# A two-layer encoder on one core: the taps of a depthwise convolution move between two engines, and the first weights are rounded on another one

## The chip, the core and the metric

The kernel runs on one core of a Trainium2 chip. The core has a matrix engine (TensorE, in the profile PE, with its weight loads as PEld), a vector engine (VectorE, DVE), an engine for functions of one operand (ScalarE, ACT), a general engine (GpSimd, POOL) and a queue for transfers (SyncE, SP). Each engine works through its own queue of instructions in a fixed order and waits where it needs something from another one. The metric is device time in microseconds, from the start of the program to its end; the median of three runs counts.

## The reference, cut to what matters

Two layers, 256 tokens, 2048 channels, float32. The attention part (two head groups and one output projection) is the same before and after. The change lies in the second half of each layer:

```python
def depthwise_conv(u, w, bias):                 # u: (1, 256, 11264), w: (3, 11264)
    up = jnp.pad(u, ((0, 0), (1, 1), (0, 0)))
    return up[:, :-2] * w[0] + up[:, 1:-1] * w[1] + up[:, 2:] * w[2] + bias

h2 = rms_norm(x, ln2_g[l])
u = depthwise_conv(h2 @ w_up[l], conv_w[l], conv_b[l])
gate, up = u[..., :D_FF], u[..., D_FF:]         # D_FF = 5632
x = x + (jax.nn.silu(gate) * up) @ w_down[l]
```

## The kernel before, in words

**Weights in two parts.** Every float32 weight tile (`raw`, 128x2048, 1 MB) comes in by a transfer on SP's queue and is split in two halves of 1024 columns. ACT rounds a half to a high part `whi` (line 112), DVE subtracts this from the weight to get the low part `wlo` (line 113), and PE multiplies with both. `split_w` (line 752) does this four steps ahead of PE (`SPLIT_AHEAD`), with five buffers for each part: the rounding of a step can start when PE has left the buffer of five steps before. `x` and all other activations are split in the same way (lines 112 to 117; `mid` tiles hold both parts of one activation).

**The feed-forward half of a layer.** The 5632 hidden channels are 44 pieces of 128 (gate and up together). A piece is made by two weight tiles (`q_up`, line 527), four steps of PE, and then `glu` (line 541) on the other engines: ACT copies one half of the result out of PSUM (545), DVE adds the other half (546) and scales it by the row norm into a tile `halo` with room for the neighbours (547), POOL copies the two edges (549, 550). The convolution is next: ACT computes the middle tap with the bias, once for the gate and once for up (555), and DVE adds the two neighbours' taps to each, four instructions with multiply and add in one (557). ACT applies SiLU (559), DVE multiplies with the other half (561), and the result is split into a `mid` tile (563). After every second piece `sums_mid` (570) makes sums and differences of the two (574 to 577) and splits those too.

**Five groups of pieces.** The pieces go in groups of 8, 8, 8, 8 and 12 (`CHUNKS`). After the ninth `q_up` of a group comes `q_plain` (639), whose result DVE adds to `x` (654), and then four times a `seven` tile followed, in the first four groups, by a `down` tile. A `seven` tile holds four weight blocks of a product that is built from seven block products; its three parts are split in `split_seven` (743), where DVE first combines the blocks in place (747, 748, 749): part 1 needs 747, part 2 needs 749. So with every `seven` tile ACT waits for DVE, DVE for ACT, and PE for both.

**What sets the order.** The code is recorded by a framework whose scheduler sorts the instructions of each engine by its own estimate of their times and by priorities; `split_w` has a priority ahead of the other work. An engine's order can therefore move far from an edit. Buffers: `pT` tiles (`y` in `glu`) are four in turn.

**The start.** `head` (norm weights and the first two blocks of x transposed) and the next two blocks come on ACT's queue, the first weight tile in four parts and the second one on SP's queue. ACT rounds the blocks of x (`first_x`, line 786, by way of 115) and the first weights (112), each in program order.

Of the kernel before, what the change touches and what calls it, by code (L numbers as in the profile page):

```python
# [11 lines left out]
F32 = mybir.dt.float32  # L12
F32R = mybir.dt.float32r
I32 = mybir.dt.int32
AF = mybir.ActivationFunctionType
ALU = mybir.AluOpType
AX = mybir.AxisListType

P = 128
L = 2  # L20
T = 256
# [10 lines left out]
NF = FF // P  # L32
# [27 lines left out]
def encoder_kernel(  # L60
# [5 lines left out]
    nc = tc.nc  # L66
# [3 lines left out]
    work = ctx.enter_context(tc.tile_pool(name="work", bufs=2))  # L70
# [38 lines left out]
    def split(hi, lo, src, scale=None):  # L109

        if scale is None:
            high = nc.scalar.activation(hi, src, AF.Copy)  # L112
            nc.vector.tensor_sub(lo, src, hi.bitcast(F32))  # L113
        else:
            high = nc.scalar.activation(hi, src, AF.Copy, scale=scale)  # L115
            nc.vector.scalar_tensor_tensor(lo, src, scale, hi.bitcast(F32),
                                           op0=ALU.mult, op1=ALU.subtract)
        return high
# [10 lines left out]
    def prep_x(l, which, k, src):  # L129

        xs[k] = act.tile([P, 2, T], F32R, name=f"xs{k}")
        split(xs[k][:, 0], xs[k][:, 1], src, ln_g[:, which, l, k:k + 1])
# [385 lines left out]
    def middle(l, f):  # L518

        name, bufs = "mid", MIDS  # L520
        if f >= NF - CHUNKS[-1]:
            k = count[l] = count.get(l, 0) + 1
            if k > MIDS:
                name, bufs = SPARE[k - MIDS - 1]
        return act.tile([P, 2, T], F32R, name=name, bufs=bufs)

    def q_up(l, f, u):
        def body(q, half, hi, lo):
            if u == 0 and half == 0:
                cur["up"] = psum.tile([P, 2, 2, T], F32, name="mm", bufs=2)  # L530
            ps = cur["up"]
            hv, lv = (w.rearrange("p (k j n) -> p k j n", k=4, j=2) for w in (hi, lo))
            for j in range(2):
                for kk in range(4):
                    k = 8 * u + 4 * half + kk
                    two(ps[:, j], hv[:, kk, j], lv[:, kk, j], xs[k], k == 0, k == KD - 1)
            if u == 1 and half == 1:
                glu(l, f, ps)
        return body

    def glu(l, f, ps):
        ux = halo[f % 2]
        r = T // GRID_W
        t = work.tile([P, 2, T], F32, name="prob", bufs=2)
        nc.scalar.activation(t, ps[:, :, 0], AF.Copy)  # L545
        nc.vector.tensor_add(t, t, ps[:, :, 1])  # L546
        nc.vector.tensor_mul(ux[:, :, r:r + T], t, st["r2"][:, None, :].to_broadcast([P, 2, T]))  # L547

        nc.gpsimd.tensor_copy(ux[:, :, 1:r], ux[:, :, T:T + r - 1])  # L549
        nc.gpsimd.tensor_copy(ux[:, :, T + r:T + 2 * r - 1], ux[:, :, r + 1:2 * r])  # L550
        y = work.tile([P, 2, T], F32, name="pT", bufs=4)
        for j in range(2):
            c = j * NF + f
            w0, w1, w2, b = (par["conv"][:, l, i, c:c + 1] for i in range(4))
            nc.scalar.activation(y[:, j, :], ux[:, j, r:r + T], AF.Identity, scale=w1, bias=b)  # L555
            for w, o in ((w0, 0), (w2, 2 * r)):
                nc.vector.scalar_tensor_tensor(y[:, j, :], ux[:, j, o:o + T], w, y[:, j, :],  # L557
                                               op0=ALU.mult, op1=ALU.add)
        nc.scalar.activation(t[:, 0, :], y[:, 0, :], AF.Silu)  # L559
        m = work.tile([P, T], F32, name="bias", bufs=2)  # L560
        nc.vector.tensor_mul(m, t[:, 0, :], y[:, 1, :])
        gs[f] = middle(l, f)
        split(gs[f][:, 0], gs[f][:, 1], m)
        ms[f] = m
        if f % 2 and f < NF - CHUNKS[-1] + PART:
            sums_mid(l, f // 2, ms.pop(f - 1), ms.pop(f))
# [3 lines left out]
    def sums_mid(l, p, m1, m2):  # L570

        a, b = slice(0, P), slice(P, T)
        v = work.tile([P, 4, HD], F32, name="tq", bufs=2)
        nc.vector.tensor_add(v[:, 0], m1[:, b], m2[:, b])
        nc.vector.tensor_sub(v[:, 1], v[:, 0], m1[:, a])
        nc.vector.tensor_sub(v[:, 2], m1[:, a], m1[:, b])
        nc.vector.tensor_sub(v[:, 3], m2[:, a], v[:, 1])
        for i in range(2):
            t = middle(l, 2 * p)
            split(t[:, 0], t[:, 1], v[:, 2 * i:2 * i + 2].rearrange("p j n -> p (j n)"))  # L580
            for j in range(2):
                ss[p, 2 * i + j] = t[:, :, j * P:(j + 1) * P]
# [116 lines left out]
    for l in range(L):  # L699
# [7 lines left out]
        f = 0  # L707
# [25 lines left out]
    raw, hl, left, loads, highs = {}, {}, {}, {}, {}  # L733

    def load(q, parts=1):
        if q < len(quanta):
            raw[q] = wp.tile([P, 2048], F32, name="raw", bufs=3)
            left[q] = 3 if quanta[q][2] == "seven" else 2
            m = 2048 // parts
            for j in range(parts):  # L740
                loads[q] = nc.sync.dma_start(out=raw[q][:, j * m:(j + 1) * m], in_=quanta[q][0][:, j * m:(j + 1) * m])

    def split_seven(w, part, hi, lo):

        hv, lv = (t.rearrange("p (k n) -> p k n", k=2) for t in (hi, lo))
        if part == 1:
            nc.vector.tensor_sub(w[:, 1:3], w[:, 1:3], w[:, 2:4])
            nc.vector.tensor_add(w[:, 3], w[:, 3], w[:, 1])
            nc.vector.tensor_sub(w[:, 0], w[:, 3], w[:, 0])
        return split(hv, lv, (w[:, 1::2], w[:, 1:3], w[:, 0::3])[part])  # L750

    def split_w(s, parts=1):
        if s < len(steps):
            q, half = steps[s]
            kind = quanta[q][2]
            o = UP_AT if kind == "up" else 0
            hl[s] = tuple(wp.tile([P, 1024 + 64], F32R, name=t, bufs=SPLIT_AHEAD + 1)[:, o:o + 1024]
                          for t in ("whi", "wlo"))
            with tc.high_priority(offset=AHEAD_PRIO if s >= KD // 2 else 0):
                if kind == "seven":  # L760
                    highs[s] = split_seven(raw[q].rearrange("p (k n) -> p k n", k=4), half, *hl[s])
                else:
                    m = 1024 // parts
                    for j in range(parts):
                        highs[s] = split(*(t[:, j * m:(j + 1) * m] for t in hl[s]),
                                         raw[q][:, half * 1024 + j * m:half * 1024 + (j + 1) * m])
            left[q] -= 1
            if left[q] == 0:
                del raw[q]
                load(q + LOAD_AHEAD)  # L770
# [15 lines left out]
    def first_x(i):  # L786
        for j in range(2):
            prep_x(0, 0, 2 * i + j, xT[i][:, j, :])
# [7 lines left out]
    par = {}  # L796
# [37 lines left out]
        mm(ps[:, 0:P], ones, ones, True, True)  # L834

    for i in range(SPLIT_AHEAD):
        first_x(i)
        split_w(i, 2 if i == 0 else 1)
    for n, shape, dt, src in (
            ("pos", [P, TT], I32, a["pos"]),  # L840
            ("inv", [P, HD // 2], F32, a["inv"].partition_broadcast(P))):
# [11 lines left out]
    for s, (q, half) in enumerate(steps):  # L853
        if s + SPLIT_AHEAD < KD // 2:
            first_x(s + SPLIT_AHEAD)
        split_w(s + SPLIT_AHEAD)
        quanta[q][1](q, half, *hl.pop(s))
        for f, args in side.pop((q, half), []):
            f(*args)
# [101 lines left out]
```

## Time and profile before

| | us |
|---|---|
| median of three runs | 2092.12 |
| lowest and highest | 2092.11, 2092.13 |
| the profiled execution, its own time | 2092.0 |
| its span, first to last instruction | 2090.2 |
| PE busy in the span | 2083.5 |
| DVE busy | 1720.5 |
| ACT busy | 1222.3 |
| POOL busy | 170.3 |

The span is read from left to right; a window of it is given in microseconds from its start. The granted clock of PE is 1.00 over the whole span. One feed-forward half has five groups that look alike in the trace: nine pieces of `q_up`, in which DVE and ACT have much idle time, and then some 34 us of `q_plain`, `seven` and `down`, in which DVE is nearly always busy. A row of a timeline gives start, busy time, engine, line, operation, what it writes and reads, and in brackets the idle time before it and what ended that; neighbouring instructions of one kind are merged with their count.

### The profile page before, as it was taken

Reading aid. Unit: us, or ns where it says so; the run is one execution under the profiler, and the core shown is the slowest. Engines: PE = TensorE matmul, PEld = TensorE weight load, DVE = VectorE, ACT = ScalarE, POOL = GpSimd, SP = SyncE. Lnnn points to the kernel's source line nnn. Section 1 sums busy time; section 2 is a strip of 40 time slices with the busy share of each in tenths; the row PEclk is TensorE's granted clock in tenths of the full one; section 3 lists DMA queues with packets and bytes.
Section 4 is the critical chain, followed back from the end, with each engine's and each line's share of the span. In section 5 each row is a group of like instructions: output and inputs, shape, how many; then the busy total and the mean of one; then the engine's idle time right before and its main releaser. Section 6 shows DMA issues by size and latency. Waiting matters only on the chain.

```text
span 2090.2 us, 29185 instructions
## 1 busy us (share of the span) xinstructions
PE 2083.5 (100%) x10816; PEld 1789.2 (86%) x10816; DVE 1720.5 (82%) x2604; ACT 1222.3 (58%) x1817; POOL 170.3 (8%) x237
## 2 busy tenths in 40 slices
PE   9999999999999999999999999999999999999999
PEld 8888888888888888888888888888888888888887
DVE  7786757898898988989757866678989989899896
ACT  7566556555555556556555665565556555555563
POOL 0011100100101001010000011001001010010100
PEclk9999999999999999999999999999999999999999
DMA  9544555556565564655655444555555655556554
GB/s 350 199 145 164 179 172 174 198 195 211 180 241 182 208 210 167 242 193 211 208 181 181 162 160 166 177 182 189 214 202 170 236 199 204 201 185 234 185 200 161
DMA packets 62144, 408.42 MB, mean 195 GB/s; under 512 B 7344, under 2 KB 9904, under 8 KB 13744
## 3 DMA queue, kind: packets, MB, share of 16 engines
q1 hardware_dynamic: 61280, 405.46, 56.2%
q8 instruction: 85, 1.39, 0.3%
q10 hardware_dynamic: 720, 1.08, 0.2%
q14 instruction: 59, 0.48, 0.1%
HBM read 404.42 MB, written 2.10 MB: 194 GB/s over the span
## 4 chain that ended last, share of the span: by engine, by line
PE 99%; DMA 0%; ACT 0%; DVE 0%; issue 0%
PE mm L98 90%; PE S L98 4%; PE pv L98 3%; PE tr L98 2%; PE tr L373 1%; PE tr L307 1%; PE S L149 1%; DMA head<-in_head 0%; ACT qtok L274 0%; ACT kT L315 0%; ACT xs L115 0%; DVE x L688 0%; ACT whi L112 0%
## 5 line engine op out<-in xcount | busy, mean ns | idle before, releaser
L112 ACT ACTIVATE whi<-raw 128x1024 fp32r<-128x1024 f32 (+1 forms) x797 | 830.9, 1057 | 689.9 <-PE mm L98 411.9
L113 DVE TENSOR_TENSOR wlo<-raw,whi 128x1024 fp32r<-128x1024 f32 (+1 forms) x797 | 963.9, 1220 | 270.3 <-ACT whi L112 231.8
L98 PE MATMUL mm<-xs,whi 128*128 128x512 f32 x2816 | 977.0, 390 | 0.0
L98 PE MATMUL mm<-xs,wlo 128*128 128x256 f32 x2816 | 794.1, 282 | 0.0
L98 PEld LDWEIGHTS mm<-xs,whi 128*128 128x128 f32 x2816 | 528.3, 188 | 110.5
L98 PEld LDWEIGHTS mm<-xs,wlo 128*128 128x128 f32 x2816 | 532.2, 189 | 1.1
L98 PE MATMUL mm<-whi,mid 128*128 128x512 f32 x1412 | 368.2, 391 | 0.0
L98 PEld LDWEIGHTS mm<-whi,mid 128*128 128x128 f32 x1412 | 263.0, 188 | 53.9
L98 PE MATMUL mm<-whi,xs 128*128 128x512 f32 x1152 | 294.2, 393 | 1.4 <-ACT qtok L274 1.3
L98 PEld LDWEIGHTS mm<-whi,xs 128*128 128x128 f32 x1152 | 213.1, 188 | 44.7 <-ACT qtok L274 1.8
L98 PE MATMUL mm<-wlo,mid 128*128 128x512 f32 x706 | 202.4, 392 | 0.0
L98 PE MATMUL mm<-wlo,xs 128*128 128x512 f32 x576 | 159.5, 393 | 0.0
L98 PEld LDWEIGHTS mm<-wlo,mid 128*128 128x128 f32 x706 | 132.1, 188 | 27.0
L557 DVE SCALAR_TENSOR_TENSOR pT<-halo,conv,pT 128x256 f32<-128x256 f32 x352 | 148.1, 478 | 0.9
L549 POOL COPY halo<-halo 128x6 f32<-128x6 f32 x88 | 39.6, 450 | 1232.6 <-DVE halo L547 1232.6
L98 PEld LDWEIGHTS mm<-wlo,xs 128*128 128x128 f32 x576 | 107.3, 188 | 21.6
L555 ACT ACTIVATE pT<-halo,conv 128x256 f32<-128x256 f32 x176 | 95.1, 587 | 5.8 <-DVE halo L547 5.7
L550 POOL COPY halo<-halo 128x6 f32<-128x6 f32 x88 | 77.1, 876 | 0.2 <-POOL halo L549 0.2
L547 DVE TENSOR_TENSOR halo<-prob,acc_b 128x512 f32<-128x512 f32 x88 | 60.6, 689 | 1.9
L546 DVE TENSOR_TENSOR prob<-prob,mm 128x512 f32<-128x512 f32 x88 | 59.8, 679 | 0.0
L545 ACT ACTIVATE prob<-mm 128x512 f32<-128x512 f32 x88 | 51.3, 583 | 7.1 <-PE mm L98 7.1
L559 ACT ACTIVATE prob<-pT 128x256 f32<-128x256 f32 x88 | 35.5, 404 | 30.0 <-DVE pT L557 30.0
(180 smaller groups left out, 1475.4 us busy)
## 6 DMA issues: line engine op xcount, KB each, us to landing
raw<-in_w_up SPq DMA_DIRECT2D x176, 1024.0 KB, 4.9
raw<-in_w_in SPq DMA_DIRECT2D x71, 1024.0 KB, 4.9
raw<-in_w_down SPq DMA_DIRECT2D x48, 1024.0 KB, 4.8
raw<-in_w_seven SPq DMA_DIRECT2D x40, 1024.0 KB, 4.9
raw<-in_w_out SPq DMA_DIRECT2D x32, 1024.0 KB, 4.9
raw<-in_w_plain SPq DMA_DIRECT2D x10, 1024.0 KB, 4.8
bias<-in_bias SPq DMA_DIRECT2D x16, 160.0 KB, 3.1
x<-in_x SPq DMA_DIRECT2D x4, 512.0 KB, 10.7
```

What stands on the lines that cost most here:

```text
L98: nc.tensor.matmul(ps, lhsT, rhs, start=start, stop=stop, skip_group_check=True)
L112: high = nc.scalar.activation(hi, src, AF.Copy)
L113: nc.vector.tensor_sub(lo, src, hi.bitcast(F32))
L149: nc.tensor.transpose(ps[:, j, tt * P:(tt + 1) * P], x[:, tt, (k + j) * P:(k + j + 1) * P], ident)
L545: nc.scalar.activation(t, ps[:, :, 0], AF.Copy)
L546: nc.vector.tensor_add(t, t, ps[:, :, 1])
L547: nc.vector.tensor_mul(ux[:, :, r:r + T], t, st["r2"][:, None, :].to_broadcast([P, 2, T]))
L549: nc.gpsimd.tensor_copy(ux[:, :, 1:r], ux[:, :, T:T + r - 1])
L550: nc.gpsimd.tensor_copy(ux[:, :, T + r:T + 2 * r - 1], ux[:, :, r + 1:2 * r])
L555: nc.scalar.activation(y[:, j, :], ux[:, j, r:r + T], AF.Identity, scale=w1, bias=b)
L557: nc.vector.scalar_tensor_tensor(y[:, j, :], ux[:, j, o:o + T], w, y[:, j, :], op0=ALU.mult, op1=ALU.add)
L559: nc.scalar.activation(t[:, 0, :], y[:, 0, :], AF.Silu)
```

## The change

The neighbours' taps: ACT now multiplies each tap by its weight (four instructions of 256 columns in a piece), into two further `pT` tiles `z`, and DVE adds a whole `z` (gate and up, 512 columns) to `y` in one instruction, twice in a piece. Before, DVE did four instructions of 256 columns. The very first weight half: DVE rounds it (two copies of 512 columns) instead of ACT, and ACT's rounding of the first two blocks of x stands after these in the program.

```diff
+        w = [[par["conv"][:, l, i, j * NF + f:j * NF + f + 1] for i in range(4)] for j in range(2)]
         for j in range(2):
-            c = j * NF + f
-            w0, w1, w2, b = (par["conv"][:, l, i, c:c + 1] for i in range(4))
-            nc.scalar.activation(y[:, j, :], ux[:, j, r:r + T], AF.Identity, scale=w1, bias=b)
-            for w, o in ((w0, 0), (w2, 2 * r)):
-                nc.vector.scalar_tensor_tensor(y[:, j, :], ux[:, j, o:o + T], w, y[:, j, :],
-                                               op0=ALU.mult, op1=ALU.add)
+            nc.scalar.activation(y[:, j, :], ux[:, j, r:r + T], AF.Identity, scale=w[j][1], bias=w[j][3])
+        for i, o in ((0, 0), (2, 2 * r)):
+            z = work.tile([P, 2, T], F32, name="pT", bufs=4)
+            for j in range(2):
+                nc.scalar.activation(z[:, j, :], ux[:, j, o:o + T], AF.Copy, scale=w[j][i])
+            nc.vector.tensor_add(y, y, z)
         nc.scalar.activation(t[:, 0, :], y[:, 0, :], AF.Silu)
...
-                    m = 1024 // parts
-                    for j in range(parts):
-                        highs[s] = split(*(t[:, j * m:(j + 1) * m] for t in hl[s]),
-                                         raw[q][:, half * 1024 + j * m:half * 1024 + (j + 1) * m])
+                    w = raw[q][:, half * 1024:(half + 1) * 1024]
+                    if s == 0:
+                        m = [slice(j * 512, (j + 1) * 512) for j in range(2)]
+                        for j in m:
+                            highs[s] = nc.vector.tensor_copy(hl[s][0][:, j], w[:, j])
+                        first_x(0)
+                        with tc.issue_after(highs[s].ins):
+                            for j in m:
+                                nc.vector.tensor_sub(hl[s][1][:, j], w[:, j], hl[s][0][:, j].bitcast(F32))
+                    else:
+                        highs[s] = split(*hl[s], w)
```

In the changed kernel's line numbers the middle tap is 554, a neighbour's tap on ACT 559, DVE's addition 560, SiLU 561, the product 563; `q_plain`'s addition is 656 and the three block combinations are 749, 750 and 751.

The scheduler also gives other orders at the end of each group. **DVE, from the addition of the ninth piece's two halves to the combinations of the second `seven` tile.** `prob` and `halo` are the ninth piece's, `x<-x,mm` is `q_plain`'s addition, `tq` and `mid` the sums of pieces seven and eight. Before:

```order
L546 TENSOR_TENSOR prob<-prob,mm 128x512
L113 TENSOR_TENSOR mid<-tq,mid 128x256
L547 TENSOR_TENSOR halo_110<-prob,acc_b 128x2x256
L113 TENSOR_TENSOR wlo<-raw,whi 128x1024
L654 TENSOR_TENSOR x<-x,mm 128x512
L113 TENSOR_TENSOR wlo<-raw,whi 128x1024
L113 TENSOR_TENSOR mid<-tq,mid 128x256
L113 TENSOR_TENSOR wlo<-raw,whi 128x1024
L557 SCALAR_TENSOR_TENSOR pT<-halo_110,conv,pT 128x256 x2
```

Now:

```order
L546 TENSOR_TENSOR prob<-prob,mm 128x512
L113 TENSOR_TENSOR mid<-tq,mid 128x256
L656 TENSOR_TENSOR x<-x,mm 128x512
L547 TENSOR_TENSOR halo_110<-prob,acc_b 128x2x256
L113 TENSOR_TENSOR wlo<-raw,whi 128x1024 x3
L113 TENSOR_TENSOR mid<-tq,mid 128x256
L113 TENSOR_TENSOR wlo<-raw,whi 128x1024
L560 TENSOR_TENSOR pT<-pT 128x512
```

`q_plain`'s addition to `x`, which waits for PE, now stands ahead of 547 and of the low part of the first `seven` tile's last part.

**DVE, the rows that follow, through the second `seven` tile.** Before:

```order
L113 TENSOR_TENSOR wlo<-raw,whi 128x1024
L557 SCALAR_TENSOR_TENSOR pT<-halo_110,conv,pT 128x256 x2
L747 TENSOR_TENSOR raw<-raw 128x1024
L561 TENSOR_TENSOR bias<-prob,pT 128x256
L748 TENSOR_TENSOR raw<-raw 128x512
L749 TENSOR_TENSOR raw<-raw 128x512
L113 TENSOR_TENSOR wlo<-raw,whi 128x1024
```

Now:

```order
L749 TENSOR_TENSOR raw<-raw 128x1024
L560 TENSOR_TENSOR pT<-pT 128x512
L750 TENSOR_TENSOR raw<-raw 128x512
L113 TENSOR_TENSOR wlo<-raw,whi 128x1024
L751 TENSOR_TENSOR raw<-raw 128x512
L563 TENSOR_TENSOR bias<-prob,pT 128x256
```

The last combination (749 before, 751 now), for which part 2's rounding waits, now stands behind a low part of 1024 columns.

**PE, parts 1 and 2 of that second `seven` tile.** `whi_4131` and `whi_4144` are the high parts of parts 1 and 2 before, `whi_4167` and `whi_4180` now; `wlo_4132` and `wlo_4168` are part 1's low parts. Before:

```order
L98 MATMUL S_4112<-whi_4131,mid_3534 128x512 x2
L98 MATMUL S_4111<-whi_4131,mid_3531 128x512 x2
L98 MATMUL pv_4114<-whi_4144,mid_3523 128x512 x2
L98 MATMUL mm_4110<-whi_4144,mid_3531 128x512 x2
L98 MATMUL S_4112<-wlo_4132,mid_3534 128x512
```

Now:

```order
L98 MATMUL S_4148<-whi_4167,mid_3550 128x512 x2
L98 MATMUL S_4147<-whi_4167,mid_3547 128x512 x2
L98 MATMUL S_4148<-wlo_4168,mid_3550 128x512
L98 MATMUL S_4147<-wlo_4168,mid_3547 128x512
L98 MATMUL pv_4150<-whi_4180,mid_3539 128x512 x2
```

The two products with part 1's low part now come ahead of part 2's first product.

## Rows read from the trace of the kernel before

**Rows 1.** The page, part 1: engine, busy us (share of the span), instructions.

```profile
PE 2083.5 (100%) x10816; PEld 1789.2 (86%) x10816; DVE 1720.5 (82%) x2604; ACT 1222.3 (58%) x1817; POOL 170.3 (8%) x237
```

**Rows 2.** Waits of PE: who waited for whom, us, times, longest.

```profile
PE mm L98 <- ACT qtok L274: 1.3, 2, 0.7
PE pv L98 <- DVE halfpi L94: 1.1, 1, 1.1
```

**Rows 3.** Busy time by window; columns PE, PEld, DVE, ACT, POOL, clock, DMA.

```profile
434.00:468.00 34.00, 34.00 (x152) 28.15 (x151) 33.63 (x37) 20.08 (x24) 1.18 (x2) 1.00 0.58 208
468.00:564.00 96.00, 96.00 (x546) 84.66 (x545) 84.23 (x129) 56.25 (x81) 8.76 (x15) 1.00 0.58 201
```

**Rows 4.** Chain that ended last, in order of time: the first pieces of two groups.

```profile
467.87 94.66 PE mm L98 x538
...
597.44 94.66 PE mm L98 x538
```

**Rows 5.** Groups by line and form: the removed taps, the nearest form on ACT.

```profile
L557 DVE SCALAR_TENSOR_TENSOR pT<-halo,conv,pT 128x256 f32<-128x256 f32 x352 | 148.1, 478 | 0.9
L115 ACT ACTIVATE xs<-mid,head 128x256 fp32r<-128x256 f32 x14 | 6.0, 495 | 0.1
```

**Rows 6.** Timeline of DVE, eighth piece of a group, up to its `seven` tile.

```profile
424.81 1.67 DVE L557 SCALAR_TENSOR_TENSOR pT<-halo,conv,pT 128x256 f32<-128x256 f32 x4
426.43 1.23 DVE L113 TENSOR_TENSOR wlo<-raw,whi 128x1024 fp32r<-128x1024 f32 x1
```

**Rows 7.** Timeline of ACT there, the middle taps and the next rounding.

```profile
423.54 1.08 ACT L555 ACTIVATE pT<-halo,conv 128x256 f32<-128x256 f32 x2
425.34 1.06 ACT L112 ACTIVATE whi<-raw 128x1024 fp32r<-128x1024 f32 x1 [0.72 <-ACT pT L555]
```

**Rows 8.** Timeline of POOL there: the edges.

```profile
423.69 1.26 POOL L550 COPY halo<-halo 128x6 f32<-128x6 f32 x1
```

**Rows 9.** Timeline of DVE, from the ninth piece's scaling to the second `seven` tile.

```profile
433.26 0.68 DVE L547 TENSOR_TENSOR halo<-prob,acc_b 128x512 f32<-128x512 f32 x1
433.86 1.22 DVE L113 TENSOR_TENSOR wlo<-raw,whi 128x1024 fp32r<-128x1024 f32 x1
435.00 0.68 DVE L654 TENSOR_TENSOR x<-x,mm 128x512 f32<-128x512 f32 x1
435.60 1.22 DVE L113 TENSOR_TENSOR wlo<-raw,whi 128x1024 fp32r<-128x1024 f32 x1
436.73 0.42 DVE L113 TENSOR_TENSOR mid<-tq,mid 128x256 fp32r<-128x256 f32 x1
437.07 1.22 DVE L113 TENSOR_TENSOR wlo<-raw,whi 128x1024 fp32r<-128x1024 f32 x1
...
443.11 0.69 DVE L749 TENSOR_TENSOR raw<-raw 128x512 f32<-128x512 f32 x1
```

**Rows 10.** Timeline of PE: end of `q_plain`, then parts 1 and 2.

```profile
433.71 0.62 PE L98 MATMUL mm<-wlo,mid 128*128 128x512 f32 x2
...
444.36 1.07 PE L98 MATMUL S<-whi,mid 128*128 128x512 f32 x4
445.27 0.62 PE L98 MATMUL pv<-whi,mid 128*128 128x512 f32 x2
```

**Rows 11.** Timeline of ACT: roundings of part 2 and of three more.

```profile
443.92 3.91 ACT L112 ACTIVATE whi<-raw 128x1024 fp32r<-128x1024 f32 x4 [0.32 <-DVE raw L749]
```

**Rows 12.** DMA issues in the window 1.75 to 2.05: KB, us to landing.

```profile
mid<-in_xT ACTq DMA_DIRECT2D x1, 256.0 KB, 6.4
```

**Rows 13.** Timeline of the whole core at the start: issue, PE's first two steps, ACT.

```profile
1.72 0.39 ACTq L781 DMA_DIRECT2D mid<-in_xT  x1
...
6.74 2.42 PE L98 MATMUL mm<-whi,xs 128*128 128x512 f32 x8
...
8.91 1.05 ACT L112 ACTIVATE whi<-raw 128x1024 fp32r<-128x1024 f32 x1
...
10.01 2.11 PE L98 MATMUL mm<-whi,xs 128*128 128x512 f32 x8
```

More of the change, by code (lines that the diff above doesn't have):

```diff
@@ L750, in split_seven, with split_w @@
         return split(hv, lv, (w[:, 1::2], w[:, 1:3], w[:, 0::3])[part])
-    def split_w(s, parts=1):
+    def split_w(s):
         if s < len(steps):
@@ L836, in encoder_kernel @@
     for i in range(SPLIT_AHEAD):
-        first_x(i)
-        split_w(i, 2 if i == 0 else 1)
+        if i > 0:
+            first_x(i)
+        split_w(i)
     for n, shape, dt, src in (
```

## The prediction

> **What bounds the kernel now.** I read the page's busy times first: PE is busy for 2083.5 of 2090.2 us, VectorE for 1720.5, ScalarE for 1222.3 [rows 1]. A busy PE need not be a PE at its peak, so I looked at what it waits for: two waits, 2.4 us in all, neither of them for a convolution [rows 2]. The chain in order of time says the same: two neighbouring groups of pieces begin at 467.87 and 597.44, a period of 129.57 us, each with the same unbroken 94.66 us of matmuls [rows 4]. PE is the bound from end to end. Time can therefore be gained only at the two ends of the program, and lost wherever a prepared weight comes too late for PE.
>
> So the question is how much lead the weights have. The windows show two stages. In the 96 us in which a group's pieces are multiplied, VectorE is busy for 84.23 and ScalarE for 56.25: both have time over. In the 34 us of `q_plain`, `seven` and `down`, VectorE is busy for 33.63 of 34.00 [rows 3]. There it is as good as full, and there the lead is thin: part 2 of the second `seven` tile is rounded by ScalarE from 443.92, right after VectorE's combination 749 (443.11 for 0.69, so to 443.80), is ready at 444.98 (1.06, rows 7), and PE starts on it at 445.27 [rows 9 to 11]. That is a lead of 0.29 us. It comes once in each of the first four groups of a layer, eight times in all; the order of the instructions is the same in these eight, before and after.
>
> **The change part by part.**
>
> *The first weights.* Before, ScalarE rounded the two blocks of x and then the weights, and PE's first step began at 6.74. With VectorE's copies the weights come alongside the blocks; PE might be through with this step some 0.5 us sooner (the first product follows the warming-up matmuls, the second no longer waits for a second rounding of 0.5 us). But PE's second step began at 10.01, right behind ScalarE's rounding of its weights (8.91 for 1.05, so to 9.96), and that rounding stands behind blocks of x whose transfer was issued at 1.72 and took 6.4 us, so to 8.1 [rows 12, 13]. Two roundings of 0.41 follow that landing in both kernels, then the weights. PE's second step stays at 10.0: gain 0. The cover is the transfer; without it the gain would be 0.5 us, once.
>
> *The taps in a piece.* VectorE gives up four instructions that held it for 1.62 us (424.81 to 426.43) [rows 6]. It gets two additions of 512 columns; the nearest rows are 547 and 654, which hold it for 0.60 each (433.26 to 433.86, 435.00 to 435.60) [rows 9]. It saves 0.4 us a piece. ScalarE gets four multiplications of 256 columns; the nearest row lasts 0.495 [rows 5], and consecutive ones overlap, so I take 0.41 each, bounds 0.40 and 0.59 (the middle taps, 1.08 for two with an overlap of 0.10) [rows 7]: 1.6 us a piece. In the 96 us of a group's pieces both sums fit into idle time. Where PE does not wait, what VectorE saves is worth nothing, and what ScalarE adds costs nothing.
>
> The Trainium skill, "ScalarE: Activation LUTs", Rules for kernel authors, would have multiplications on VectorE and not on ScalarE. The rows bear it out only weakly, 478 ns against 495 for a tap [rows 5]; by that rule alone the sum would change by nothing that PE sees.
>
> *The chain at the eighth piece.* What the edit lengthens is a chain. Before, VectorE went from the taps straight on to the first `seven` tile's low part at 426.43. Now ScalarE's middle taps (from 423.54, free at 424.52) are followed by the four neighbours' taps, to 426.16, and only then by the rounding that this low part needs: 427.22 (1.06). POOL's edges end at 424.95 [rows 8], before the third tap wants them. VectorE stands at 427.25 where it stood at 426.43, so 0.82 us late, in spite of its saving. From there on it is full, so the ninth piece's 547 would come at 434.08 instead of 433.26.
>
> *The moved addition.* In the new order `q_plain`'s addition to x stands ahead of 547, and it needs the end of `q_plain` on PE: 433.71 and 0.62, so 434.33 [rows 10]. With 0.04 for the signal, VectorE is held there until 434.37. Queued behind it are 547 and four low parts; before, the addition came later and never waited. From 434.37 I add up what stands in the order, each by the time for which its row holds the engine: addition 0.60, 547 0.60, three low parts of 1.14 (433.86 to 435.00), a `mid` 0.34 (436.73 to 437.07), one more low part 1.14, a conv addition 0.60, the first combination (1024 columns, as a low part) 1.14, the other conv addition 0.60, the second combination 0.60 [rows 9]. That makes 443.4. ScalarE's six instructions on this piece are done by 441, since 547 ends at 435.6. The next low part waits for part 1's rounding, which follows the first combination (441.07, 1.22) by 0.1 for the signal, as 749 to its rounding [rows 9, 11], and takes 1.06: 443.48. Then 1.14 for this low part, 0.69 for the third combination: 445.3. ScalarE's rounding of part 2 runs from 445.4 to 446.46, and with 0.05 PE can start at 446.51.
>
> When does PE want it? It wanted it at 445.27; now two products of part 1 stand ahead, 0.227 us each (four take from 444.36 to 445.27) [rows 10], so at 445.72. **PE stalls for 0.79 us.** The next rounding on ScalarE follows 0.96 later (four in 3.91), four matmuls on PE take 0.91: another 0.05. All later parts have leads of 0.4 us or more by the same count, and a stalled PE widens them. So 0.84 us a group, and eight groups make 6.7 us.
>
> The sum: the profiled execution took 2092.0, that is its span of 2090.2 and 1.8 around it; 2092.0 + 6.7 = 2098.7, and the median of the three runs is 0.1 above this execution: **2098.8 us**.
>
> The bounds of the unknown prices: a conv addition lies between 0.33 (half of 547's 0.60, and the fixed part) and 0.87 (what a merged pair of the removed taps takes at most, two of 478 less their overlap of 0.08). Two stand in the chain, so 0.84 turns into 0.3 to 1.4 a group, 2.4 to 11 us in all. I take 0.60, as it is a row of the same operation and size. Slower taps (0.59) would bring VectorE to the addition 0.7 later, at 434.8, and add 0.4; faster ones change nothing, since it waits there anyway.
>
> **The rivals.**
>
> *No change: VectorE's saving covers the chain.* Place: the stretch between the end of `q_plain` and part 2's rounding. VectorE is full there [rows 3], and what is taken off it brings that rounding forward. Price 0: 2092.1. It decides where the stretch from 434.37 to the end of the third combination takes 10.1 us instead of 10.9; two additions of 0.2 us would do it, or a held addition that starts 0.8 sooner. For it: before, the same stretch left 0.29 over. Against it: both additions would have to run three times as fast as the rows of their size, and the hold ends with a matmul whose place is fixed. The Trainium skill, "Perfetto Trace Analysis", Optimizing Scalar/DVE Operations, speaks for this side: it says that offloading a saturated VectorE to ScalarE may make sense. The trace agrees on the saturation, in the 34 us; by that rule the sum would be 2092.1, as PE had nothing to wait for.
>
> *Twice the stall: ScalarE's queue is held.* Place: the six instructions in a row on ScalarE in the eighth and ninth pieces, behind which roundings are queued, and the wait for POOL's edges that the first of the taps now has. Price: with 0.59 a tap, and the first tap held until POOL's 424.95, VectorE reaches the addition at some 435.1, 0.7 later; 0.84 + 0.7 is 1.5 a group, 12 us: 2104. It decides where the eighth piece's taps end after 426.5. Against it: in the trace 256 columns on ScalarE mostly take less than the middle taps, and an instruction waits for one edge at a time.
>
> *The start alone counts.* If ScalarE's second weights did not wait for x, 0.5 us would be gained: 2091.6 without a stall. The landing speaks against it.
>
> **How the numbers follow.** A measurement of this kernel can tell about 0.2%, 4.2 us, from no change; slower by more begins at 2096.3, 0.53 us a group. My forecast has 0.66, and its own range is 2095 to 2102.5; a tenth of it lies below 2096.3. No change has 0.20, the held queue 0.09, and 0.05 is left for what I do not see, part of it a gain. Slower by over 0.2%: 0.60 + 0.09 + 0.01, so 0.70. Within 0.2%: 0.20 + 0.06 + 0.01, so 0.27. Faster: 0.03. The range reaches down to the no-change case and up to a group's 1.3 us: 2092.0 to 2102.5.
>
> **What would show it.** In the waits of PE there should be a new one, for the rounding of `whi`, some eight times and 6 us in total; in the chain, groups with a period of 130.4 us. VectorE's plain addition at 656 should have idle time before it, ended by PE. VectorE's busy time should fall by some 35 us, ScalarE's rise by 145. PE's second step should begin at 10.0 as before. I am wrong if the period stays at 129.6: then look at what a 560 takes, and whether VectorE waits at 656. I am wrong in size if the stall is elsewhere than at part 2 of the second `seven` tile.

## The result and the profile after

The changed kernel takes 2101.14 us (median of five runs; 2100.70 to 2101.65) against 2092.12: a ratio of 1.0043, 95% interval 1.0028 to 1.0058. It is slower by 9.0 us, where 6.7 were forecast. The profiled execution took 2100.93, of which the span is 2098.5; span and surroundings grew by 8.3 and 0.6 us.

The page of the kernel after, part 1 (engine, busy us, share, instructions), answers to [rows 1]:

```profile
PE 2086.7 (99%) x10816; PEld 1788.1 (85%) x10816; DVE 1689.2 (80%) x2430; ACT 1361.4 (65%) x2167; POOL 173.4 (8%) x237
```

VectorE gave up 31.3 us (some 35 were forecast), ScalarE took on 139.1 (145). The two new groups of instructions, by line:

```profile
L559 ACT ACTIVATE pT<-halo,conv 128x256 f32<-128x256 f32 x352 | 149.9, 497 | 4.3 <-POOL halo L549 1.9
L560 DVE TENSOR_TENSOR pT<-pT 128x512 f32<-128x512 f32 x176 | 121.6, 691 | 63.4 <-ACT pT L559 55.4
```

The waits of PE have two more rows than [rows 2]. The one with 0.3 us lies in the start. The other has eight occurrences, as many as there are groups before each layer's last (some 6 us were forecast for it; why it shows only 4.8 is told in the last section):

```profile
PE pv L98 <- ACT whi L112: 4.8, 8, 0.6
PE mm L98 <- ACT qtok L274: 1.3, 2, 0.7
PE pv L98 <- DVE halfpi L94: 1.1, 1, 1.1
PE mm L98 <- ACT whi L112: 0.3, 1, 0.3
```

The chain of the kernel after, in order of time, gives the price of one occurrence. Two neighbouring groups [rows 4]:

```profile
469.05 94.21 PE mm L98 x536
...
599.54 94.21 PE mm L98 x536
```

That is a period of 130.49 us against 129.57, so 0.92 a group. This trace also runs a little late; just ahead of the stalling place, the first product of part 1 stands at 444.58 where it stood at 444.36, so I take 0.22 off when I compare times there.

The timeline of VectorE in the kernel after, from the eighth piece to the third combination [rows 6, 9]:

```profile
425.64 1.49 DVE L560 TENSOR_TENSOR pT<-pT 128x512 f32<-128x512 f32 x2 [0.57 <-ACT pT L559]
427.39 1.23 DVE L113 TENSOR_TENSOR wlo<-raw,whi 128x1024 fp32r<-128x1024 f32 x1 [0.26 <-ACT whi L112]
...
434.58 0.69 DVE L656 TENSOR_TENSOR x<-x,mm 128x512 f32<-128x512 f32 x1 [0.28 <-PE mm L98]
435.19 0.69 DVE L547 TENSOR_TENSOR halo<-prob,acc_b 128x512 f32<-128x512 f32 x1
435.79 3.49 DVE L113 TENSOR_TENSOR wlo<-raw,whi 128x1024 fp32r<-128x1024 f32 x3
...
443.68 1.22 DVE L113 TENSOR_TENSOR wlo<-raw,whi 128x1024 fp32r<-128x1024 f32 x1
444.82 0.69 DVE L751 TENSOR_TENSOR raw<-raw 128x512 f32<-128x512 f32 x1
```

ScalarE's taps and its roundings of parts 1 and 2 [rows 7, 11]:

```profile
424.71 1.70 ACT L559 ACTIVATE pT<-halo,conv 128x256 f32<-128x256 f32 x4
...
442.58 1.06 ACT L112 ACTIVATE whi<-raw 128x1024 fp32r<-128x1024 f32 x1 [2.58 <-DVE raw L749]
...
445.60 3.90 ACT L112 ACTIVATE whi<-raw 128x1024 fp32r<-128x1024 f32 x4 [1.65 <-DVE raw L751]
```

And PE there [rows 10]:

```profile
444.58 1.07 PE L98 MATMUL S<-whi,mid 128*128 128x512 f32 x4
445.49 0.61 PE L98 MATMUL S<-wlo,mid 128*128 128x512 f32 x2
446.71 0.73 PE L98 MATMUL pv<-whi,mid 128*128 128x512 f32 x2 [0.61 <-ACT whi L112]
```

Read backwards: PE waits for part 2's rounding, the rounding for the third combination 751, and 751 stands behind part 1's low part in a queue that reaches back to 434.58, where VectorE waited for PE to end `q_plain`. The only gap in it is 0.07 us ahead of that low part, which at 443.68 waits for part 1's rounding, as that one waits for the first combination (749, 441.27 to 442.49).

### The profile page after: what moved, and what is told of

The parts are those of the page before. It is cut to its first block, busy times and chain, and to the rows that moved or that the text cites. A ratio compares the mean times of both kernels' runs of the same rounds, so it can differ in the third digit from the quotient of the medians.

```text
span 2098.5 us, 29319 instructions
## 1 busy us (share of the span) xinstructions
PE 2086.7 (99%) x10816; PEld 1788.1 (85%) x10816; DVE 1689.2 (80%) x2430; ACT 1361.4 (65%) x2167; POOL 173.4 (8%) x237
## 4 chain that ended last, share of the span: by engine, by line
PE 97%; DVE 1%; ACT 1%; issue 0%; DMA 0%; ACTq 0%; DVEq 0%
PE mm L98 88%; PE S L98 3%; PE pv L98 3%; PE tr L98 1%; PE tr L373 1%; PE tr L307 1%; PE S L149 0%; ACT whi L112 0%; DVE wlo L113 0%; DMA mid<-in_xT 0%; DVE raw L751 0%; DVE pT L560 0%; ACT qtok L274 0%; DVE halo L547 0%; DVE raw L750 0%
## 5 line engine op out<-in xcount | busy, mean ns | idle before, releaser
L112 ACT ACTIVATE whi<-raw 128x1024 fp32r<-128x1024 f32 x795 | 827.0, 1056 | 575.7 <-PE mm L98 389.0
L113 DVE TENSOR_TENSOR wlo<-raw,whi 128x1024 fp32r<-128x1024 f32 x795 | 961.2, 1222 | 248.8 <-ACT whi L112 212.2
L560 DVE TENSOR_TENSOR pT<-pT 128x512 f32<-128x512 f32 x176 | 121.6, 691 | 63.4 <-ACT pT L559 55.4
L559 ACT ACTIVATE pT<-halo,conv 128x256 f32<-128x256 f32 x352 | 149.9, 497 | 4.3 <-POOL halo L549 1.9
L554 ACT ACTIVATE pT<-halo,conv 128x256 f32<-128x256 f32 x176 | 95.9, 592 | 11.4 <-DVE halo L547 10.9
```

The lines of the kernel that those rows point to most:

```text
L559: nc.scalar.activation(z[:, j, :], ux[:, j, o:o + T], AF.Copy, scale=w[j][i])
L560: nc.vector.tensor_add(y, y, z)
```

## The experiments

Three theories stood against each other. **Mine:** the change lets VectorE enter the full 34 us late (a longer chain through ScalarE, then a held addition), and the order inside passes the delay on to part 2. **Rival 1:** VectorE or ScalarE has simply too much to do there, whatever the order. **Rival 2:** the first weights cost part of it. That ScalarE's taps wait for one of the four `pT` buffers, of which a piece now takes three, shows in no row: before its neighbour taps (559) ScalarE is idle for 4.3 us in all, and neither at 424.71 nor in the ninth piece is there a gap.

### One part of the change at a time

The changed kernel was run again beside two kernels with half of the change each.

> The changed kernel once more, on the chip of the three that follow. If the stall sits at one place of the order (the rounding of part 2 of the second seven tile, and a small one at each layer's fifth group), the groups again have a period of 130.49 us, and the time is 9.0 us above the kernel before, within 0.5. If the share that the groups do not explain (0.2 us in the start, 0.6 us outside the span) was chance, it is 8 us and PE's second step begins at 10.0 instead of 10.24.

With the convolution alone, the start is as it was:

```diff
...
-        if i > 0:
-            first_x(i)
-        split_w(i)
+        first_x(i)
+        split_w(i, 2 if i == 0 else 1)
```

> The kernel before with the change to the convolution alone; the first weights are rounded by ScalarE as before. Theory (the stall is the convolution's): the groups have a period of 130.49 us, PE waits 4.8 us for whi at 8 places, the time is 8 to 9 us above the kernel before, and within 0.4 of the changed kernel on the same chip. Rival (the new start costs the 0.2 us by which PE's second step came later, and the 0.6 us outside the span): this kernel is 0.8 us below the changed kernel, and PE's second step begins at 10.0.

With the first weights alone, the taps stay on VectorE:

```diff
...
-                nc.scalar.activation(z[:, j, :], ux[:, j, o:o + T], AF.Copy, scale=w[j][i])
-            nc.vector.tensor_add(y, y, z)
+                nc.vector.scalar_tensor_tensor(y[:, j, :], ux[:, j, o:o + T], w, y[:, j, :],
+                                               op0=ALU.mult, op1=ALU.add)
```

> The kernel before with the change to the first weights alone. Theory (the second step hangs on a block of x that lands at about 8.1 us): PE's second step begins within 0.1 of the kernel before when set against that landing, the groups keep 129.57 us, and the time is within 0.3 us of the kernel before. Rival (the start alone counts): PE's second step begins at 9.5 and the time is 0.5 us below the kernel before. Second rival (the start itself costs): 0.2 to 0.8 us above.

Measured: 2100.95, 2100.95 and 2092.36 us, against 2092.26 for the kernel before on the same chip. The intervals of the ratios are 1.0030 to 1.0055, 1.0029 to 1.0056 and 0.9992 to 1.0009. The convolution is all of it and rival 2 falls. The changed kernel has its period again (130.48) and lies 8.7 us above the kernel before. With the convolution alone, PE waits for `whi` at eight places, 4.8 us, and the period is that of the whole change (469.14 to 599.63, 130.49).

In the start only the landing of the late block of x moves PE's second step: it lands at 8.07, 8.42, 8.30, 8.14 and 7.99 us in the kernel before, with the convolution alone, with the whole change twice, and with the first weights alone, and the step begins at 10.01, 10.36, 10.24, 10.07 and 9.92. That is 1.93 or 1.94 later each time, whichever engine rounds the first weights. The 0.2 us that the first profiled execution of the changed kernel lost in the start was a late landing. The second step is not all of the start, though: with the first weights alone it begins 0.09 sooner than in the kernel before, and yet the groups stand 0.41 later (468.28 against 467.87). The chain of that kernel goes through a weight tile that landed at 28.11.

### The held addition, behind 547

```diff
-        nc.vector.tensor_mul(ux[:, :, r:r + T], t, st["r2"][:, None, :].to_broadcast([P, 2, T]))
+        cur["scaled"] = nc.vector.tensor_mul(ux[:, :, r:r + T], t, st["r2"][:, None, :].to_broadcast([P, 2, T]))
...
-                nc.vector.tensor_add(xv, xv, ps)
+                with tc.issue_after(cur["scaled"].ins):
+                    nc.vector.tensor_add(xv, xv, ps)
```

> The changed kernel with q_plain's addition to x issued behind the multiplication 547, so that VectorE has 547 to do while PE ends q_plain. Theory (the addition is held, 0.28 us before it in the trace of the changed kernel, and everything behind it shifts by that): VectorE has no idle time there, part 2's rounding comes 0.28 us sooner, the period falls from 130.49 to 130.2, the time by 2.2 us. Rival (the hold costs nothing, since the chain from the taps through ScalarE sets when part 2 is rounded): the period stays at 130.49. Second rival (the hold is the whole of it): 129.57 and the time of the kernel before.

Measured: 2097.76 us (1.0016 to 1.0038), 3.2 us less than the changed kernel where I expected 2.2. The period is 130.13 by its chain, and VectorE's queue has the addition (657) and the third combination (752) here:

```profile
468.53 84.19 PE mm L98 x480
...
598.66 84.19 PE mm L98 x480
```
```profile
434.09 0.68 DVE L547 TENSOR_TENSOR halo<-prob,acc_b 128x512 f32<-128x512 f32 x1
434.69 0.68 DVE L657 TENSOR_TENSOR x<-x,mm 128x512 f32<-128x512 f32 x1
...
444.32 0.69 DVE L752 TENSOR_TENSOR raw<-raw 128x512 f32<-128x512 f32 x1
```

The addition follows 547 without a wait. In the changed kernel it could have followed the `mid` ahead of it at 434.22 (433.88 in its timeline, and 0.34) and began at 434.58, a hold of 0.36 (I had expected the 0.28 that its row shows as idle time, but a row lasts 0.08 longer than the next one has to wait); the period fell by just that, from 130.49 to 130.13. Both rivals to this run fall (that the hold costs nothing, that it is everything), and 0.56 a group is still to be explained.

### Half of the taps, as many additions

This kernel leaves out one neighbour of the convolution.

```diff
-        for i, o in ((0, 0), (2, 2 * r)):
-            z = work.tile([P, 2, T], F32, name="pT", bufs=4)
-            for j in range(2):
-                nc.scalar.activation(z[:, j, :], ux[:, j, o:o + T], AF.Copy, scale=w[j][i])
+        z = work.tile([P, 2, T], F32, name="pT", bufs=4)
+        for j in range(2):
+            nc.scalar.activation(z[:, j, :], ux[:, j, 0:T], AF.Copy, scale=w[j][0])
+        for _ in range(2):
             nc.vector.tensor_add(y, y, z)
```

> The changed kernel with ScalarE making only one neighbour's taps, which VectorE adds twice: the convolution's other neighbour is left out. VectorE has as many instructions as in the changed kernel, and at the group's end its queue stands as in the kernel whose addition stands behind 547, but for one short mid; ScalarE's chain to the first seven tile's low part is two taps, 0.8 us, shorter. Theory (the chain through ScalarE makes VectorE enter the full stretch 0.82 us late): VectorE comes to 547 at 433.3, the addition behind it is then held for 0.5 until q_plain's end, so the period is 129.8 to 129.9 against 130.14, and the time 2 us below that kernel, 2094.5 to 2095.5. Rival (VectorE's own additions are what is too much): 130.14 and the time of that kernel, 2097.8. Second rival (the chain is all): 129.57.

Measured: 2095.24 us (1.0006 to 1.0024), a period of 129.90 (468.21 to 598.11). Both lie in what the chain theory gave, though VectorE does the same work here as in the kernel above. The steps were a little off. VectorE, at three places:

```profile
426.77 1.22 DVE L113 TENSOR_TENSOR wlo<-raw,whi 128x1024 fp32r<-128x1024 f32 x1
...
433.60 0.68 DVE L547 TENSOR_TENSOR halo<-prob,acc_b 128x512 f32<-128x512 f32 x1
434.38 0.69 DVE L656 TENSOR_TENSOR x<-x,mm 128x512 f32<-128x512 f32 x1
```

The low part begins at 426.77 instead of 427.26 (0.5 sooner and not 0.82, since now VectorE's own two additions end just ahead of it), and the addition behind 547 is held for 0.18 and not 0.5 (433.60 and 0.60 make 434.20, and it starts at 434.38). So it starts 0.31 sooner than at 434.69; 0.07 of that is the trace, which runs ahead by as much there (part 1's first product stands at 444.38 and 444.45), and the other 0.24 is the gain in the period, 0.23. The stretch from the addition's start to the third combination's end is 10.3 us in both kernels, so what counts is when VectorE may enter it.

### The low part behind the third combination

Part 1's low part stood ahead of 751. Here it is issued behind it:

```diff
-            nc.vector.tensor_sub(w[:, 0], w[:, 3], w[:, 0])
+            last = nc.vector.tensor_sub(w[:, 0], w[:, 3], w[:, 0])
+            with tc.issue_after(last.ins):
+                return split(hv, lv, w[:, 1:3])
```

> The changed kernel with part 1's low part issued behind the third combination 751, which part 2's rounding waits for; in the new order one low part also stands ahead of q_plain's addition, so that VectorE is not held there, and PE takes part 2's first products ahead of part 1's low ones. Theory (part 2's rounding is late because VectorE's queue has a hold and a low part ahead of 751): from the kernel whose addition stands behind 547, where 751 ends 445.00 behind a low part of 1.14, 751 comes at 443.2 and the rounding ends at about 444.95, while PE wants it at 445.25; no stall, a period of 129.57 us, a time within 0.5 us of the kernel before, though ScalarE still makes all the taps. Rival (any order stalls, as VectorE has too much to do in the 34 us): the stall moves to part 1's low part or to later parts, and the period stays above 130.

Measured: 2103.79 us (1.0042 to 1.0070), a period of 130.57 (469.10 to 599.67). My theory missed by over 11 us, and by the time alone rival 1 would be right. The trace of this kernel shows something else, first on POOL, then ScalarE, then VectorE:

```profile
436.72 3.66 POOL L549 COPY halo<-halo 128x6 f32<-128x6 f32 x1 [11.65 <-DVE halo L547]
```
```profile
440.42 1.71 ACT L559 ACTIVATE pT<-halo,conv 128x256 f32<-128x256 f32 x4 [2.69 <-POOL halo L549]
```
```profile
435.91 0.68 DVE L547 TENSOR_TENSOR halo<-prob,acc_b 128x512 f32<-128x512 f32 x1
436.51 2.35 DVE L113 TENSOR_TENSOR wlo<-raw,whi 128x1024 fp32r<-128x1024 f32 x2
438.78 0.42 DVE L113 TENSOR_TENSOR mid<-tq,mid 128x256 fp32r<-128x256 f32 x1
439.12 1.22 DVE L113 TENSOR_TENSOR wlo<-raw,whi 128x1024 fp32r<-128x1024 f32 x1
441.36 0.69 DVE L560 TENSOR_TENSOR pT<-pT 128x512 f32<-128x512 f32 x1 [1.02 <-ACT pT L559]
```

POOL's copy of the ninth piece's edges, six columns, takes 3.66 us. It ends at 440.38, when VectorE's run of four subtractions behind 547 ends (439.12 and 1.22, so 440.34). ScalarE's neighbour taps wait for the edge, VectorE for the taps, and the 1.02 us lost there eat the gain of the order. In this kernel, as in the changed one, the addition stands ahead of 547, so that nothing but subtractions follows 547. Besides, PE waited twice, 1.3 us each, for VectorE's line 546 in the layers' fifth groups; that is most of the 2.8 us by which this kernel is slower than the changed one.

### Both orders

The edit is the two above together: low part behind the third combination, addition behind 547.

> As the kernel with part 1's low part behind the third combination, but with q_plain's addition behind 547 instead of ahead of it; nothing else stands otherwise on VectorE in the 34 us. Theory, formed after that kernel's trace (POOL's edge copy of 128x6 took 3.66 us there, from 436.72 to 440.38, as long as VectorE ran low parts, which read two tiles of SBUF; in the kernel whose addition stands behind 547 it took 0.19 beside the addition, which reads PSUM): both copies take under 0.25 us behind 547, the neighbours' taps follow the middle ones, the first 560 does not wait, 751 ends at about 443.9 and part 2's rounding at 445.0, which is before PE wants it; a period of 129.57 us and 2092.0 to 2092.6. Rival (the low part behind 751 is itself what stalls): the period stays at about 130.6 and the time at 2103.8.

Measured: 2092.44 us against 2092.16 (0.9993 to 1.0010). The chain's groups are 129.57 us apart. Its rows, POOL's copies and VectorE in this kernel:

```profile
468.20 94.21 PE mm L98 x536
...
597.77 94.21 PE mm L98 x536
```
```profile
436.28 0.19 POOL L549 COPY halo<-halo 128x6 f32<-128x6 f32 x1 [11.05 <-DVE halo L547]
436.40 0.19 POOL L550 COPY halo<-halo 128x6 f32<-128x6 f32 x1
```
```profile
436.06 0.68 DVE L657 TENSOR_TENSOR x<-x,mm 128x512 f32<-128x512 f32 x1
...
443.47 0.69 DVE L752 TENSOR_TENSOR raw<-raw 128x512 f32<-128x512 f32 x1
444.08 1.22 DVE L113 TENSOR_TENSOR wlo<-raw,whi 128x1024 fp32r<-128x1024 f32 x1
```

and ScalarE and PE at part 2:

```profile
444.25 2.96 ACT L112 ACTIVATE whi<-raw 128x1024 fp32r<-128x1024 f32 x3 [0.56 <-DVE raw L752]
```
```profile
445.60 0.62 PE L98 MATMUL pv<-whi,mid 128*128 128x512 f32 x2
```

ScalarE still makes every tap, and the kernel is level with the one before. The rounding ends at 445.31 (444.25 and 1.06), the lead is again 0.29 us, and PE waits for no rounding in the groups. Rival 1 falls: there is room in the 34 us; it was the order that let the stall in.

### The start, for a gain

Where PE's second step comes later or sooner, what follows mostly moves with it (the kernel with the first weights alone is the exception), so I let ScalarE round its weights ahead of the late blocks of x: in the kernel before, in the one with the low part moved, and in the one with both orders. The edit to the latter two (in the kernel before, the four steps are written out to the same end):

```diff
-        if i > 0:
+        if i == 2:
+            with tc.issue_after(highs[1].ins):
+                first_x(i)
+        elif i > 0:
             first_x(i)
```

> The kernel before with its roundings in the start reordered: ScalarE rounds the weights of PE's second step ahead of the blocks of x that land at 8.1. Theory (the second step waits only for this rounding): the rounding ends at 8.7 or sooner, PE's second step begins 0.4 us sooner, at about 9.6, behind the first step's products, and the time falls by 0.4 us, to 2091.9. Rival (the products of the first step need the blocks that land last and end at about 9.9): the step begins as before and the time stays.

> The changed kernel with both: part 1's low part behind the third combination, and ScalarE's rounding for PE's second step ahead of the late blocks of x. If the two act apart, the time is that of the kernel with the first alone less 0.4 us, 2091.9, level with the kernel before or just below it. Rival (the start is set by the landing): the same as with the first alone, 2092.3.

> The same, with ScalarE's rounding for PE's second step ahead of the late blocks of x in the start. If the two act apart: 0.2 to 0.3 us less than without it, 2091.8 to 2092.3, which is level with the kernel before within what can be told. Rival (the start costs a wait later, since the blocks of x come later): the same time or 0.2 more.

Measured: 2091.89 against 2092.10 (0.9990 to 1.0008); 2103.55, where the same without the start took 2103.79; 2092.23, where the same without it took 2092.44. Each is 0.2 us lower, too little to tell from nothing. The second missed its 2091.9 with the order that it was built on. In the first of them ScalarE and PE show why it is not 0.4:

```profile
8.72 1.06 ACT L112 ACTIVATE whi<-raw 128x1024 fp32r<-128x1024 f32 x1 [0.73 <-DMA raw<-in_w_in]
```
```profile
9.45 0.62 PE L98 MATMUL mm<-wlo,xs 128*128 128x512 f32 x2
9.90 0.67 PE L98 MATMUL mm<-whi,xs 128*128 128x512 f32 x2
```

The rounding no longer stands behind x, but its weights land at 8.63, 0.6 us after the late block, so it ends at 9.78 and not at 8.7. Nor is it the last thing that PE waits for: the first step's last two products, 0.227 us each from 9.45 on, end their turn at 9.90, and the second step begins right there. Against 10.01 there was 0.1 us to gain. So the first step's products set this start, as the rival to this run had it, and the rounding does not.

No kernel was found that is measurably faster than the one before.

## Why the prediction was right, and where it was off

**Right: the bound and the place.** PE is the bound, VectorE's saving of 31.3 us brought nothing, and the new wait is at part 2 of the second `seven` tile, eight times.

**Right: the chain, the hold and the order.** Less the 0.22 us, VectorE comes to the low part at 427.17 (forecast 427.25), the held addition starts at 434.36 (434.37), 751 ends at 445.29 (445.3), and PE starts on part 2 at 446.49 (446.51). It wanted it 0.227 after the last low product began (445.49 and 0.23, so 445.72, and 0.23): 445.95, less 0.22 is 445.73, as forecast (445.72). The experiments bear out the two causes: the hold 0.36 a group, the chain at least 0.23 (130.13 to 129.90), and the order inside the stretch decides whether they reach PE at all (129.57 with both moved).

**Right: the prices.** A conv addition holds VectorE for 0.60 (440.67 to 441.27, the start of the next row), though its row lasts 691 ns; four taps take 1.70 and end at 426.41, less 0.22 at 426.19 (forecast 426.16).

**Right: the start.** It is worth nothing, since the second step hangs on the late block. The 0.5 us that it was said to be worth without that block are not borne out: with the weights rounded ahead of it, in the two kernels with the new start, the second step begins at 9.79 and 9.74, because the weights themselves land at 8.59 and 8.53.

**Off: the size of a stall, 0.92 and not 0.84.** The wait itself was 0.76 (446.71 less 445.95; forecast 0.79). The step that failed is the small one behind it. I had given 0.05 to the next rounding, but that was there in time (lead 0.14). Instead the first products after the wait are slower: the two of part 2 take 0.73 where they took 0.62 [rows 10], at a granted clock of 1.00 in both traces. That is 0.11, and a few hundredths more are spread over the next ones. Eight times 0.08 is 0.6 us. The size of this term was wrong, not the mechanism.

**Off: the fifth groups were left out.** The addition is held there too, 0.28 us at 956.58 in the timeline of VectorE, and PE has no thick lead behind it: from the fifth group's pieces to the next layer's, 524.17 us pass instead of 523.86 (860.52 to 1384.69, 856.57 to 1380.43), and the end comes 192.8 behind the last group instead of 192.4. The low part that follows there (957.78, two in 2.35, to 960.13) is ready 0.06 before PE's product at 960.19, so close that no wait shows. That makes another 0.6 us. With the addition alone moved it is 523.88 (858.92 to 1382.80), so there it was the hold; at the second layer's end that kernel waits 0.5 us for line 546 instead. With both orders moved the 523.86 are back (856.90 to 1380.76).

**Not in the sum: the landing and what lies around the span.** The landing gave 0.2, by chance, as shown. Around the span lie 1.8 us in the kernel before, with the first weights alone and with half of the taps 1.8 to 1.9, and 2.0 to 2.5 in the seven kernels with all taps on ScalarE; it is 2.4 to 2.5 in all three profiles with the held addition ahead of 547 and the low part unmoved. So these 0.6 us may well belong to the change, though not to the first weights; what they are stays open. 6.7 and 0.6, 0.6, 0.2, 0.6 make 8.7 of the 8.9 us between the two profiled executions.

**Off, without consequence: the lower bound.** Two cheaper additions were taken to save twice. But by the forecast's own steps the second one stands beside part 1's rounding, which follows the first combination; only the first one is on the way to part 2, as the 0.07 us gap at 443.68 bears out. At 0.33 each the forecast stall would have been 0.57 a group and not 0.3.

**The rivals.** "VectorE's saving covers the chain" had a fair deciding point: the stretch took 10.9 us (434.58 to 445.51), not 10.1, so it did not. (Two additions of 0.2 us would not have done it either, for the reason just given.) The Trainium skill's "Perfetto Trace Analysis", Optimizing Scalar/DVE Operations, which spoke for that side, says that offloading a saturated VectorE to ScalarE may make sense. In these runs it cost 9 us, and with both orders moved it cost nothing and brought nothing (2092.44 against 2092.16). "Twice the stall" needed taps that end after 426.5; they ended at 426.41 even in the late trace. Yet a held ScalarE queue was no fancy: in the kernel with the low part moved it was held for 2.69 us by POOL's edges, the mechanism that I named; but that was at the ninth piece, and I had priced it only at the eighth.

## What to carry to other kernels

Where one engine is the bound, work that is taken off another is worth nothing, but the chain that it is moved into can cost: follow the first consumer of every moved result, and price what stands behind it in each queue up to the bound. A scheduler that works with estimated times may turn such an edit into another order, so look for an instruction that now stands ahead of others and waits for the bound engine; two edits of the order gave back all of the 9 us here. And mend an order with the trace of the mended kernel in hand: the move of the low part alone cost another 2.8 us, the move of the addition alone gave back 3.2.

## What was not expected of the hardware

**POOL's copy waits for VectorE's subtractions.** The 128x6 copy takes 0.19 us beside VectorE's addition, which reads one tile and PSUM, and up to 3.66 beside low parts, which read two tiles. In the changed kernel it lies between:

```profile
436.00 1.05 POOL L549 COPY halo<-halo 128x6 f32<-128x6 f32 x1 [10.89 <-DVE halo L547]
437.00 1.20 POOL L550 COPY halo<-halo 128x6 f32<-128x6 f32 x1
```

They end at 437.05 and 438.20, each some 0.05 behind the end of a low part (435.79 and 1.22 make 437.01, the next ends 1.14 later). The Trainium skill, "SBUF — State Buffer", section "SBUF: two separate sides", has a rule for this: a VectorE instruction with two inputs in SBUF and a GpSimd instruction that reads SBUF exclude each other, and whichever starts first keeps the shared port for its whole instruction. The rows agree (0.19 us beside the addition, ends 0.05 behind those of low parts), with one thing more: in the kernel with the low part moved, the waiting copy got its turn at none of the three ends of instructions on the way (437.73, 438.86, 439.20), only at the last. Why it does at some and not at others stays open.

**The wait that the profile shows is less than what is lost.** The page has 4.8 us in eight waits, 0.60 each; the period has 0.92. A product's row lasts 0.39 us, but the next one begins 0.227 later, so the first 0.16 of a wait lies under the row before it, and the slower first products come on top. In the kernel with half of the taps PE shows no wait at all at this place, and still each group takes 0.33 longer; in the one with the addition behind 547 it shows 0.24 and loses 0.56. The difference is 0.32 or 0.33 in all three: take the period of a repeated group, not the sum of the waits.
